# The turns of a unit's rows one step later in the scan, and the later modulation blocks on VectorE

## The chip, the cores and the metric

One core of one Trainium2 chip runs the whole program in one launch. The metric is the device time of that launch in microseconds (us). Before the change it was 1558.77 us, the median of three runs (1555.15 to 1559.71).

## The reference, cut to what matters

Two transformer blocks on 256 tokens of width 1024, in float32. The first one has a modulated norm, an RWKV mixer, neighbourhood attention and 16 experts; the second has a pooling and dilated-attention mixer, a feed-forward part and a gate, twice. The change touches two pieces of the first block.

The modulation is a product of a vector with a 1024 x 6144 matrix:

```
m_x = jnp.split(jax.nn.silu(c) @ mod_w[l] + mod_b[l], 6, axis=-1)
```

Its last four sixths are needed only behind the mixers.

The RWKV mixer runs a delta-rule scan in two directions, over 256 context tokens and then 256 latent ones, for 8 heads of 64:

```
s_kk = jnp.einsum('bhvk,bhk->bhv', s, kk_t)
s = (s * w_t[:, :, None, :]
     - s_kk[..., None] * (kk_t * a_t)[:, :, None, :]
     + v_t[..., None] * k_t[:, :, None, :])
y = jnp.einsum('bhvk,bhk->bhv', s, inp[5]) if emit else None
```

## The kernel before, in words

The scan is done in chunks of 128 tokens. A unit is one chunk `i` (0 to 3) of one direction `d` and one group `g` of four heads: 16 units. Chunks 0 and 1 are context, 2 and 3 latent; only the latter give output (`emit`). `rwkv_prep` (L642) makes a unit's rows, with the tokens on the partitions: `rr` (L688), `nb` (L699), `kh` (L703 to L705) and, with output, `pi` (L709). `turn` (L683) brings each of them into the other orientation: two 128x128 transposes on TensorE (L686) and a copy out of PSUM on ScalarE (L687). The key scaling `kk` (L664, L665) runs on GpSimd but for first chunks. `rwkv_chunk` (L714) then multiplies the turned rows (L735, with the mask on VectorE, L739), solves a triangular system by halves (`solve`, L800; its products are L835, L841 and L844, their VectorE step L837), refines it (L869 to L880) and moves the state on.

Each unit is a generator, and a `yield` ends a step. `turns` (L48) takes one step of each live generator in a round. Three slots (`SLOTS`) of units run side by side, the second 7 rounds behind the first and the third 14 (`LEAD`); slot 0 has six units, the others five. With them run `gates` (L1015), `factors` (L325) and `rwkv_out` (L892). `gates` issues one group of gate products, L119 to L121 on weights split by L127 and L128, per round, for 160 rounds; slot 0's six units have 159 steps. A unit has 25 to 29 steps, of which `rwkv_prep` has five, or six with output.

`factors` starts with `modulation_rest` (L285): eight blocks of 512 columns, 17 steps each. A block takes eight 128x512 pieces of the matrix, each loaded by SP's queue (L299) into one of three buffers. ScalarE scales the piece by its part of the vector (L300), the first into the sum, the others in place; GpSimd adds these seven to the sum (L302). Eight small products on TensorE (L307) then sum over the partitions.

What a step issues gives the order of priority; the framework puts each engine's instructions into an order of its own, by when it reckons them ready, so that the order on an engine need not be that of the text. Each engine then takes its instructions strictly in that order. The scratch tiles `kk`, `pinv`, `pe`, `pi` and `t0` have one buffer each for all slots, the rows and their turned forms one for each slot.

Of the kernel before, what the change touches and what calls it, by code (L numbers as in the profile page):

```python
# [12 lines left out]
AF = mybir.ActivationFunctionType  # L13
ALU = mybir.AluOpType
# [57 lines left out]
class Kernel:  # L72
# [212 lines left out]
    def modulation_rest(self, pool):  # L285

        nc, a = self.nc, self.a
        self.rw = self.gp.tile([P, 8, 16], F32, name="rw")
        self.rbh = self.keep.tile([P, 16], F32, name="rb")
        nc.sync.dma_start(self.rw, a["router_w"].rearrange("(k p) e -> p k e", p=P))  # L290
        rb = a["router_bias"]
        nc.sync.dma_start(self.rbh, bass.AP(tensor=rb.tensor, offset=rb.offset, ap=[[0, P], [1, 16]]))
        nc.vector.tensor_scalar(self.rbh, self.rbh, 0.5, None, op0=ALU.add)
        w = a["mod_w"][0]
        for q in range(4, 12):
            acc = pool.tile([P, 512], F32, tag="mra", name="mra", bufs=1)
            for k in range(8):
                raw = pool.tile([P, 512], F32, tag="mr", name="mr", bufs=3)
                nc.sync.dma_start(raw, w[k * P:(k + 1) * P, q * 512:(q + 1) * 512])  # L299
                nc.scalar.activation(raw if k else acc, raw, AF.Copy, scale=self.sc[:, k, 0:1])  # L300
                if k:
                    nc.gpsimd.tensor_tensor(acc, acc, raw, op=ALU.add)  # L302
                yield
                yield
            ps = self.bank()
            for j in range(4):
                nc.tensor.matmul(ps[:, j:j + 1], acc[:, j * P:(j + 1) * P], self.ones, start=True, stop=True)  # L307
            nc.vector.tensor_tensor(self.m[:, q * 4:q * 4 + 4, 0], ps[:, 0:4], self.col["mod_b"][:, q * 4:q * 4 + 4],
                                    op=ALU.add)
            yield  # L310

        self.fac = self.keep.tile([P, 32], F32, name="fac")
        nc.vector.tensor_scalar(self.fac[:, 0:8], self.m[:, 16:24, 0], 0.5, None, op0=ALU.mult)
        nc.vector.tensor_copy(self.fac[:, 24:32], self.m[:, 40:48, 0])
        nc.vector.scalar_tensor_tensor(self.fac[:, 8:16], self.m[:, 32:40, 0], 1.0, self.col["norm2_g"], op0=ALU.add,
                                       op1=ALU.mult)
        nc.vector.tensor_copy(self.fac[:, 16:24], self.m[:, 24:32, 0])
        ps = self.bank()
        nc.tensor.transpose(ps[0:32, 0:P], self.fac, self.ident)
        row = pool.tile([32, P], F32, tag="mra", name="frow", bufs=1)  # L320
        nc.vector.tensor_copy(row, ps[0:32, 0:P])
        self.facrow = self.dram.tile([32, P], F32, name="facrow")
        nc.sync.dma_start(self.facrow[:, :], row)
# [318 lines left out]
    def rwkv_prep(self, s, d, g, t, cur, first):  # L642

        nc, pool = self.nc, self.rp
        mm = nc.tensor.matmul
        tt, stt = nc.vector.tensor_tensor, nc.vector.scalar_tensor_tensor
        emit = t < 2
        c0 = t * P
        fs = slice(256 * g, 256 * g + 256)
        tmp = lambda tag: pool.tile([P, 256], F32, tag=tag, name=tag, bufs=1)  # L650
        own = lambda shape, tag, dt=F32: self.rps[s].tile(shape, dt, tag=f"{tag}{s}", name=f"{tag}{s}", bufs=1)
        flat = lambda ap: ap.rearrange("p a b -> p (a b)")
        h4 = lambda ap: ap.rearrange("p (h n) -> p h n", h=4)

        ba = self.bank()
        mm(ba[:, 0:256], self.tl[0][d][:, c0:c0 + P], self.wlb[d][:, fs], start=True, stop=True)
        mm(ba[:, 256:512], self.tl[1][d][:, c0:c0 + P], self.alb[d][:, fs], start=True, stop=True)
        th = pool.tile([P, 512], F32, tag="th", name="th", bufs=2)
        nc.scalar.activation(th, ba, AF.Tanh, scale=0.5)
        thw, tha = th[:, 0:256], th[:, 256:512]  # L660

        kk = tmp("kk")
        eng = nc.vector if first else nc.gpsimd
        eng.tensor_tensor(kk, self.zk[t][:, fs], self.kkb[:, fs], op=ALU.mult)  # L664
        eng.tensor_tensor(h4(kk), h4(kk), self.krs[:, t, 4 * g:4 * g + 4, None].to_broadcast([P, 4, 64]), op=ALU.mult)  # L665
        yield

        bi = self.bank()
        mm(bi[:, 0:256], self.cum["i", d], thw, start=True, stop=True)
        mm(bi[:, 256:512], self.cum["e", d], thw, start=True, stop=True)  # L670
        pinv, pe = tmp("pinv"), tmp("pe")
        h = -0.5 * CDEC
        nc.scalar.activation(pe, bi[:, 256:512], AF.Exp, scale=h, bias=self.off[:, 2 * d + 1:2 * d + 2])
        nc.scalar.activation(pinv, bi[:, 0:256], AF.Exp, scale=-h, bias=self.offn[:, 2 * d:2 * d + 1])
        if emit:
            pi = tmp("pi")
            nc.scalar.activation(pi, bi[:, 0:256], AF.Exp, scale=h, bias=self.off[:, 2 * d:2 * d + 1])
        yield

        rr, nb, kh = own([P, 2, 4, 64], "rr"), own([P, 256], "nb"), own([P, 256], "kh")  # L680
        krT, nkT = own([P, 2, 2, P], "krT"), own([P, 2, 2, P], "z0")

        def turn(src, dst):  # L683
            b = self.bank()
            for p in range(2):
                nc.tensor.transpose(b[:, p * P:(p + 1) * P], src[:, p * P:(p + 1) * P], self.ident)  # L686
            nc.scalar.activation(dst, b[:, 0:256].rearrange("p (a t) -> p a t", a=2), AF.Copy)  # L687
        tt(flat(rr[:, 0]), kk, pe, op=ALU.mult)  # L688
        turn(flat(rr[:, 0]), krT[:, :, 0, :])

        bt = self.bank()
        for p in range(2):
            mm(bt[:, 2 * p:2 * p + 2], thw[:, p * P:(p + 1) * P], self.half[:, d, :], start=True, stop=True)
        hv = self.sm.tile([P, 2, 2], F32, tag=f"hv{s}", name="hv", bufs=2)
        nc.scalar.activation(hv, bt[:, 0:4].rearrange("p (a b) -> p a b", b=2), AF.Exp, scale=h, bias=self.off64)
        yield
        u = tmp("t0")
        stt(u, tha, 1.0, kk, op0=ALU.add, op1=ALU.mult)
        stt(nb, u, -0.5, pinv, op0=ALU.mult, op1=ALU.mult)  # L699
        turn(nb, nkT[:, 0])  # L700
        yield
        u = tmp("t0")
        stt(u, tha, -1.0, self.kab[:, fs], op0=ALU.add, op1=ALU.mult)  # L703
        stt(u, u, 1.0, self.zk[t][:, fs], op0=ALU.add, op1=ALU.mult)
        tt(kh, u, pinv, op=ALU.mult)  # L705
        turn(kh, nkT[:, 1])
        yield
        if emit:
            tt(pi, self.zr[t][:, fs], pi, op=ALU.mult)  # L709
            turn(pi, krT[:, :, 1, :])  # L710
            yield
        cur.update(hv=hv, rr=rr, nb=nb, kh=kh, krT=krT, nkT=nkT)

    def rwkv_chunk(self, s, d, g, t, cur, state, i, y):  # L714
# [1520 lines left out]
```

## Time and profile before

| | |
|---|---|
| median of three runs | 1558.77 us |
| profiled execution: its time, its span | 1560.86 us, 1559.1 us |
| TensorE busy, share of the span | 1471.2 us, 94% |
| VectorE busy | 867.1 us, 56% |
| ScalarE busy | 673.0 us, 43% |
| GpSimd busy | 197.4 us, 13% |
| mean granted clock of TensorE | 0.964 |

The scan takes the stretch from about 220 to 600 us. PE is TensorE's matmul, PEld its weight load, DVE is VectorE, ACT ScalarE, POOL GpSimd, SP the queue that issues loads. A granted clock of 1.00 is 2.4 GHz, 0.50 is 1.2 GHz. An instruction is named by the line of the kernel that issues it; `L686` is the transpose of all turned rows, so the tile's name tells which. Idle time is what stands between two instructions of an engine, and the profile puts it down to what ended it.

### The profile page before, as it was taken

The page shows a single profiled execution, that of the slowest core. Times are in us where ns is not written, and L with a number is a line of the kernel's source. Part 1 is how long each engine was busy: PE and PEld are TensorE (multiplying, and loading weights), DVE is VectorE, ACT ScalarE, POOL GpSimd, SP SyncE. Part 2 cuts the span into 40 slices and gives each one's busy share as a digit, 9 for nine tenths or more (in the row PEclk, how much of TensorE's full clock was granted, in tenths as well). Part 3 has the DMA queues.
Part 4 walks back from the last instruction along what each step waited for, and adds up shares of the span by engine and source line. Part 5 has one row for each costly group of instructions (what it writes and reads, how often), then busy time and mean ns, then how long its engine had stood idle before and what let it go on. Part 6 is the DMA issues. An engine that isn't in the chain of part 4 may idle for free.

```text
span 1559.1 us, 26053 instructions
## 1 busy us (share of the span) xinstructions
PE 1471.2 (94%) x10562; PEld 1122.8 (72%) x10562; DVE 867.1 (56%) x1826; ACT 673.0 (43%) x1097; POOL 197.4 (13%) x253
## 2 busy tenths in 40 slices
PE   5899999989999999789999899999999999999996
PEld 3677777878777777644443358699988887998885
DVE  3678547676666776522211245564556755755555
ACT  2433556665556553210110145554444545544443
POOL 1001123332233510058000000000000000000000
PEclk9899998898899999889999999999999999999999
DMA  9412223221222234779999925355556453555542
GB/s 326 158 46 68 68 84 116 82 82 56 68 82 83 82 119 154 306 308 420 420 419 420 393 85 187 109 188 182 181 182 202 146 189 96 175 189 189 189 162 75
DMA packets 119175, 276.29 MB, mean 177 GB/s; under 512 B 8672, under 2 KB 31876, under 8 KB 107784
## 3 DMA queue, kind: packets, MB, share of 16 engines
q1 hardware_dynamic: 115608, 270.13, 49.4%
q10 hardware_dynamic: 3407, 4.42, 0.8%
q8 instruction: 85, 1.39, 0.4%
q14 instruction: 43, 0.34, 0.1%
q0 software_dynamic: 32, 0.00, 0.0%
HBM read 272.41 MB, written 2.11 MB: 176 GB/s over the span
## 4 chain that ended last, share of the span: by engine, by line
PE 54%; DVE 1%; ACT 1%; issue 0%; DVEq 0%; ACTq 0%
PE mm L119 12%; PE mm L120 12%; PE mm L121 12%; PE mm L1546 11%; PE mm L1531 1%; PE mm L1694 1%; PE mm L1610 1%; PE mm L1951 1%; PE mm L1970 1%; PE mm L1812 1%; PE mm L1924 0%; PE mm L1980 0%; PE mm L217 0%; DVE wl L184 0%; PE mm L1913 0%
## 5 line engine op out<-in xcount | busy, mean ns | idle before, releaser
L184 DVE TENSOR_TENSOR wl<-wr,wh 128x2048 fp32r<-128x2048 f32 (+2 forms) x128 | 269.1, 2103 | 206.7 <-ACT wh L183 194.2
L183 ACT ACTIVATE wh<-wr 128x2048 fp32r<-128x2048 f32 (+2 forms) x128 | 224.9, 1760 | 156.3 <-PE mm L121 105.5
L121 PE MATMUL mm<-xTh,wl 128*128 128x256 f32 x512 | 143.9, 281 | 0.0
L120 PE MATMUL mm<-xTl,wh 128*128 128x256 f32 x512 | 143.7, 281 | 0.0
L119 PE MATMUL mm<-xTh,wh 128*128 128x256 f32 x512 | 143.3, 281 | 0.0
L119 PE MATMUL mm<-wh,fh 128*128 128x512 f32 x256 | 101.4, 396 | 0.0
L121 PE MATMUL mm<-wh,fl 128*128 128x512 f32 x256 | 101.1, 395 | 0.0
L120 PE MATMUL mm<-wl,fh 128*128 128x512 f32 x256 | 101.0, 395 | 0.0
L120 PEld LDWEIGHTS mm<-xTl,wh 128*128 128x128 f32 x512 | 96.2, 188 | 0.9 <-DVE xTl L968 0.3
L119 PEld LDWEIGHTS mm<-xTh,wh 128*128 128x128 f32 x512 | 96.1, 188 | 0.7
L119 PE MATMUL mm<-wh,xTh 128*128 128x512 f32 (+1 forms) x272 | 95.8, 352 | 0.6 <-ACT big L1888 0.4
L121 PEld LDWEIGHTS mm<-xTh,wl 128*128 128x128 f32 x512 | 96.4, 188 | 0.0
L120 PE MATMUL mm<-wl,xTh 128*128 128x512 f32 (+1 forms) x272 | 92.8, 342 | 0.0
L121 PE MATMUL mm<-wh,xTl 128*128 128x512 f32 (+1 forms) x272 | 92.6, 342 | 0.0
L302 POOL TENSOR_TENSOR mra<-mra,mr 128x512 f32<-128x512 f32 x56 | 74.3, 1327 | 54.5 <-ACT mr L300 29.6
L830 ACT ACTIVATE nt<-mm 128x512 f16<-128x512 f32 x80 | 47.2, 593 | 43.9 <-PE mm L844 38.0
L119 PEld LDWEIGHTS mm<-wh,xTh 128*128 128x128 f32 x272 | 51.2, 188 | 8.4 <-issue 0.7
L967 ACT ACTIVATE yh<-hu 128x512 fp32r<-128x512 f32 x16 | 10.1, 630 | 109.0 <-DVE hu L1602 93.8
L121 PEld LDWEIGHTS mm<-wh,fl 128*128 128x128 f32 x256 | 48.1, 188 | 11.5
L119 PE MATMUL mm<-hlh,wh 128*128 128x256 f32 x152 | 56.1, 369 | 0.0
L120 PEld LDWEIGHTS mm<-wl,fh 128*128 128x128 f32 x256 | 48.1, 188 | 10.8
L119 PEld LDWEIGHTS mm<-wh,fh 128*128 128x128 f32 x256 | 48.1, 188 | 10.7
(576 smaller groups left out, 3512.1 us busy)
## 6 DMA issues: line engine op xcount, KB each, us to landing
wr<-in_w_up_dram SPq DMA_DIRECT2D x32, 1024.0 KB, 5.7
wr<-in_w_down_dram SPq DMA_DIRECT2D x32, 1024.0 KB, 5.0
wr<-in_w_in_dram SPq DMA_DIRECT2D x22, 1024.0 KB, 5.2
wr<-in_moe_w_dram SPq DMA_DIRECT2D x21, 1024.0 KB, 13.5
wh<-in_moe_w_dram SPq DMA_DIRECT2D x20, 1024.0 KB, 13.4
wl<-in_moe_w_dram SPq DMA_DIRECT2D x20, 1024.0 KB, 14.3
mr<-in_mod_w_dram SPq DMA_DIRECT2D x64, 256.0 KB, 2.9
wx<-in_moe_w_dram SPq DMA_DIRECT2D x14, 1024.0 KB, 12.8
```

The costliest lines, as they stand in the source:

```text
L119: mm(out, l.hi, r.hi, start=start, stop=False, **kw)
L120: mm(out, l.hi, r.lo, start=False, stop=False, **kw)
L121: mm(out, l.lo, r.hi, start=False, stop=stop, **kw)
L183: self.nc.scalar.activation(w.hi, raw, AF.Copy)
L184: self.nc.vector.tensor_tensor(w.lo, raw, w.hi.bitcast(F32), op=ALU.subtract)
L302: nc.gpsimd.tensor_tensor(acc, acc, raw, op=ALU.add)
L830: nc.scalar.activation(nt, v4(bz), AF.Copy)
L1531: mm(b[:, k * 256:k * 256 + 256], part[:, t, 2 * q + k, :], sel[:, t].rearrange("p j c -> p (j c)"), start=(i == 0), stop=(i == 3))
L1546: mm(b[r], lT[:, k0 + k, c0 + SLOT * j:c0 + SLOT * j + SLOT], w[:, k], start=(start and k == 0), stop=(stop and k == n - 1))
L1610: mm(acc[2 * n + k // 2][:, k % 2], part[:, k * P:(k + 1) * P], back, start=False, stop=(g == 7 and part is y.lo), skip_group_check=True)
L1694: mm(banks[t], first[:, k, t * P:(t + 1) * P], w[:, k, :], start=(k == 0), stop=False)
L1812: nc.tensor.transpose(b[:, j * P:(j + 1) * P], self.x[:, t, 512 * n + j * P:512 * n + (j + 1) * P], self.ident)
```

## The change

In `modulation_rest` the first piece of a block is scaled on ScalarE as before. Each of the other seven is taken by one VectorE operation that scales the piece and adds it to the sum; ScalarE's scaling and GpSimd's add for it are gone.

In `rwkv_prep` each `turn` is issued in the step behind the one that makes its row. The step that makes `rr` keeps the small product and `hv`; the turn of `rr` opens the next step, which makes `nb`, and so on; the turn of the last row has a step of its own. So `rwkv_prep` has six steps, or seven with output.

```
             for k in range(8):
                 ...
-                nc.scalar.activation(raw if k else acc, raw, AF.Copy, scale=self.sc[:, k, 0:1])
                 if k:
-                    nc.gpsimd.tensor_tensor(acc, acc, raw, op=ALU.add)
+                    nc.vector.scalar_tensor_tensor(acc, raw, self.sc[:, k, 0:1], acc, op0=ALU.mult, op1=ALU.add)
+                else:
+                    nc.scalar.activation(acc, raw, AF.Copy, scale=self.sc[:, k, 0:1])
                 yield
                 yield
...
         tt(flat(rr[:, 0]), kk, pe, op=ALU.mult)
-        turn(flat(rr[:, 0]), krT[:, :, 0, :])
         ...
         nc.scalar.activation(hv, ...)
         yield
+
+        turn(flat(rr[:, 0]), krT[:, :, 0, :])
         u = tmp("t0")
         stt(u, tha, 1.0, kk, op0=ALU.add, op1=ALU.mult)
         stt(nb, u, -0.5, pinv, op0=ALU.mult, op1=ALU.mult)
+        yield
         turn(nb, nkT[:, 0])
-        yield
         u = tmp("t0")
         stt(u, tha, -1.0, self.kab[:, fs], op0=ALU.add, op1=ALU.mult)
         stt(u, u, 1.0, self.zk[t][:, fs], op0=ALU.add, op1=ALU.mult)
         tt(kh, u, pinv, op=ALU.mult)
+        yield
         turn(kh, nkT[:, 1])
-        yield
         if emit:
             tt(pi, self.zr[t][:, fs], pi, op=ALU.mult)
+            yield
             turn(pi, krT[:, :, 1, :])
-            yield
+        yield
```

## Rows read from the trace of the kernel before

**Rows 1.** Windows: length; busy us (x count) PE, PEld, DVE, ACT, POOL; clock; DMA.

```profile
220.00:560.00 340.00, 317.95 (x3751) 263.70 (x3753) 231.26 (x485) 198.64 (x421) 120.64 (x129) 0.91 0.30 88
```

**Rows 2.** Timeline, GpSimd: start, length (us), what, count, idle before and what ended it.

```profile
298.94 2.94 POOL L302 TENSOR_TENSOR mra<-mra,mr 128x512 f32<-128x512 f32 x2
...
312.62 1.26 POOL L302 TENSOR_TENSOR mra<-mra,mr 128x512 f32<-128x512 f32 x1
```

**Rows 3.** Windows over the seven clumps of adds: one of them, and their sum.

```profile
468.00:483.00 15.00, 14.17 (x181) 11.76 (x179) 10.18 (x21) 10.56 (x24) 10.80 (x10) 1.00 0.47 143
...
sum 120.00, PE 106.95 PEld 89.89 DVE 86.78 ACT 71.87 POOL 78.50; mean PE 15.28 PEld 12.84 DVE 12.40 ACT 10.27 POOL 11.21
```

**Rows 4.** Windows over seven stretches between clumps: the first, and their sum.

```profile
278.00:298.00 20.00, 19.81 (x253) 16.25 (x251) 13.27 (x33) 12.31 (x30) 2.94 (x5) 1.00 0.14 41
...
sum 155.00, PE 150.58 PEld 124.58 DVE 101.03 ACT 88.04 POOL 17.54; mean PE 21.51 PEld 17.80 DVE 14.43 ACT 12.58 POOL 2.51
```

**Rows 5.** Windows over seven stretches at low clock: the longest, and their sum.

```profile
384.00:397.60 13.60, 13.60 (x101) 10.71 (x101) 8.45 (x17) 6.90 (x15) 6.41 (x5) 0.50 0.45 134
...
sum 57.90, PE 55.49 PEld 47.27 DVE 36.44 ACT 26.56 POOL 32.37; mean PE 7.93 PEld 6.75 DVE 5.21 ACT 3.79 POOL 4.62
```

**Rows 6.** TensorE's waits, 220 to 560 us: us in total, times, longest.

```profile
PE mm L686 <- DVE kh L705: 8.1, 8, 1.9
PE mm L841 <- DVE x L837: 2.8, 4, 1.6
PE mm L121 <- DVE wl L128: 2.7, 1, 2.7
PE mm L879 <- DVE rq L876: 2.5, 2, 1.9
PE mm L686 <- DVE rr L688: 2.3, 5, 0.8
```

**Rows 7.** Two lines by themselves: ns min/median/max, first and last start.

```profile
L699 DVE SCALAR_TENSOR_TENSOR nb<-t,pinv x16: 407/422/1493, 229.4 to 548.2; 128x256 f32<-128x256 f32 x16
...
L837 DVE TENSOR_TENSOR x<-mm,lv x80: 406/424/426, 245.9 to 587.2; 128x256 f16<-128x256 f32 x80
```

**Rows 8.** Timeline of VectorE and TensorE at one stall.

```profile
300.67 1.35 DVE L629 TENSOR_TENSOR sbd<-sbd,hv 64x128 f32<-64x128 f32 x1
...
302.38 0.29 DVE L629 TENSOR_TENSOR sbd<-sbd,hv 64x128 f32<-64x128 f32 x1
...
303.28 0.66 PE L686 MATMUL mm<-ident,kh 128*128 128x128 f32 x2 [1.87 <-DVE kh L705]
```

**Rows 9.** GpSimd's groups, 220 to 560 us: busy us, mean ns; idle before.

```profile
L302 POOL TENSOR_TENSOR mra<-mra,mr 128x512 f32<-128x512 f32 x56 | 74.3, 1327 | 54.5 <-ACT mr L300 29.6 <-ACT mra L300 17.4 <-PE mm L852 5.7
L664 POOL TENSOR_TENSOR kk<-zk,kkb 128x256 f32<-128x256 f32 x12 | 9.9, 823 | 63.5 <-DVE rr L688 63.5
...
L665 POOL TENSOR_TENSOR kk<-kk,krs 128x256 f32<-128x256 f32 x12 | 8.0, 667 | 0.9
```

**Rows 10.** ScalarE's scalings among its groups, 220 to 560 us.

```profile
L300 ACT ACTIVATE mr<-mr,silu_c 128x512 f32<-128x512 f32 x56 | 39.7, 718 | 20.2 <-DMA mr<-in_mod_w_dram 18.7 <-POOL mra L302 1.5
```

**Rows 11.** VectorE's groups, 220 to 560 us.

```profile
L128 DVE TENSOR_TENSOR wl<-wr,wh 128x512 fp32r<-128x512 f32 x37 | 29.7, 803 | 12.4 <-ACT wh L127 11.3 <-ACT mr L300 0.7 <-issue 0.2
...
L703 DVE SCALAR_TENSOR_TENSOR t<-th,kab 128x256 f32<-128x256 f32 x16 | 10.6, 664 | 0.1
...
L699 DVE SCALAR_TENSOR_TENSOR nb<-t,pinv 128x256 f32<-128x256 f32 x16 | 9.6, 597 | 0.0
...
L705 DVE TENSOR_TENSOR kh<-t,pinv 128x256 f32<-128x256 f32 x16 | 8.8, 552 | 0.2
```

**Rows 12.** A line of the second block by itself: ns min/median/max.

```profile
L2114 DVE SCALAR_TENSOR_TENSOR xres<-th,xres x8: 683/692/695, 1214.9 to 1548.5; 128x512 f32<-128x512 f32 x8
```

**Rows 13.** The line that takes the gate products' results: ns, first and last start.

```profile
L1051 DVE SCALAR_TENSOR_TENSOR gt<-gt,mm x4: 680/684/689, 550.1 to 579.6; 128x512 f32<-128x512 f32 x4
```

**Rows 14.** Timeline of TensorE near the end of the last chain.

```profile
595.51 0.66 PE L779 MATMUL mm<-mk,rr 128*64 128x128 f32 x8 [0.69 <-ACT rr L880]
```

More of the change, by code (lines that the diff above doesn't have):

```diff
@@ L299, in modulation_rest @@
                 nc.sync.dma_start(raw, w[k * P:(k + 1) * P, q * 512:(q + 1) * 512])
-                nc.scalar.activation(raw if k else acc, raw, AF.Copy, scale=self.sc[:, k, 0:1])
                 if k:
-                    nc.gpsimd.tensor_tensor(acc, acc, raw, op=ALU.add)
+                    nc.vector.scalar_tensor_tensor(acc, raw, self.sc[:, k, 0:1], acc, op0=ALU.mult, op1=ALU.add)
+                else:
+                    nc.scalar.activation(acc, raw, AF.Copy, scale=self.sc[:, k, 0:1])
                 yield
@@ L688, in rwkv_prep @@
         tt(flat(rr[:, 0]), kk, pe, op=ALU.mult)
-        turn(flat(rr[:, 0]), krT[:, :, 0, :])
         bt = self.bank()
@@ L696, in rwkv_prep @@
         yield
+        turn(flat(rr[:, 0]), krT[:, :, 0, :])
         u = tmp("t0")
@@ L699, in rwkv_prep @@
         stt(nb, u, -0.5, pinv, op0=ALU.mult, op1=ALU.mult)
+        yield
         turn(nb, nkT[:, 0])
-        yield
         u = tmp("t0")
@@ L705, in rwkv_prep @@
         tt(kh, u, pinv, op=ALU.mult)
+        yield
         turn(kh, nkT[:, 1])
-        yield
         if emit:
             tt(pi, self.zr[t][:, fs], pi, op=ALU.mult)
+            yield
             turn(pi, krT[:, :, 1, :])
-            yield
+        yield
         cur.update(hv=hv, rr=rr, nb=nb, kh=kh, krT=krT, nkT=nkT)
```

## The prediction

> **What bounds the kernel now.** I began with the page's slices and chain: TensorE is busy 94% of the span, and what ends last is nearly all its matmuls, so only a stage where TensorE waits or runs at its lower clock can give time back. The change touches one such stage, the scan. In the windows by stage the reader is to see that from 220 to 560 us TensorE is busy 318.0 of 340 us, so 22.0 us idle, while its granted clock averages 0.91; VectorE is busy 231.3 us, ScalarE 198.6, GpSimd 120.6 [rows 1].
>
> Next I cut the stage where the modulation adds run on GpSimd. They come in clumps: the seven of one column block lie within 15 us on GpSimd's timeline (first and last shown) [rows 2], though the text issues one every second step, that is over some 35 us. Seven clumps, 120 us in all, hold 13.0 us of TensorE's idle time (120 less 106.95), five of them at a lowered clock; the seven stretches between them, 155 us, hold 4.4 us, all at 1.00 [rows 3, 4]. Seven stretches, 57.9 us together, run at 0.50, that is 1.2 of 2.4 GHz [rows 5]. At half clock the same columns take twice as long: of the 55.5 us of matmuls there, 27.7 would vanish at full clock. Idle time and low clock are one picture: TensorE waited for VectorE's row operations, and the clock often fell around such a wait.
>
> The waits name them: TensorE stood 8.1 and 2.3 us before the transposes of L686 for kh and rr, 10.4 of its 22.0 us [rows 6]. Why VectorE is late stands in its durations. L699, with both tensors in SBUF, takes 407 ns at best and 1493 at worst; L837, the same width with one of them in PSUM, never leaves 406 to 426 [rows 7]. The timeline of one stall shows the cause: GpSimd adds from 298.94 for 2.94 us, a 64-row scaling that takes 0.29 us at 302.38 takes 1.35 at 300.67, and TensorE has stood 1.87 us for kh when it goes on at 303.28 [rows 2, 8].
>
> **The change part by part.** The sum is made against the profiled execution, 1560.86 us (span 1559.1), which lies 2.1 us above the median of 1558.77.
>
> *The modulation adds.* GpSimd loses 56 adds, 74.3 us [rows 9]. ScalarE loses 56 scalings of 718 ns, 39.7 us [rows 10]. VectorE gains 56 operations of 128x512. The gate of the second block has the same operation on the same shape, with a constant for the vector's part and GpSimd at rest: L2114, 692 ns [rows 12]. From above, L128, also with two SBUF inputs, averages 803 with collisions in it [rows 11]. That is 38.8 to 45.0 us; I take 39 us, because the adds that stretched L128 are gone.
>
> Against it stands the time that VectorE loses to GpSimd now. Against their best of about 407 ns, L703, L699 and L705 lose 16 times 257, 190 and 145 ns, 9.5 us; L128 against L2114's 692 loses 37 times 111, 4.1 us [rows 11, 12]. Of GpSimd's two-input work the adds are 74.3 of 92.2 us (with L664 and L665) [rows 9], so I put 80% of these 13.6 us down to them, 11 us; other rows of the unit lose too, so this is a floor. Net, VectorE rises by at most 28 us, to 259 of 340, 76%. It isn't the bound on average, but in the clumps it is at 86.8 of 120 now [rows 3].
>
> The Trainium skill's page "SBUF — State Buffer", section "Who interferes with whom", says that a VectorE instruction with two SBUF inputs and a GpSimd instruction that reads SBUF exclude each other, whoever starts first; the rows agree. By the same rule the new operation, also with two SBUF inputs, collides with the key scalings that stay on GpSimd, and would be the one that speaks against this edit; those are 17.9 us of work, so by it the gain shrinks and doesn't turn.
>
> *The turns.* No instruction is added or removed: 16 units move four (or three) pairs of transposes, each with its ScalarE copy, one step later, and each unit has one step more (five become six, or six become seven where output is wanted). What it gives is slack: other work is issued ahead of the transpose while VectorE finishes the row. Bounds: nothing if the engines' order doesn't follow the text, as the clumps show that it need not, and 10.4 us if every wait goes. I take 8 us, three quarters, for a wait of 1.9 us fits into a step of about 2.1 us (340 us over some 160 steps). What is late next are the waits on L837, L128 and L876, 8.0 us together [rows 6], already with a step between; they gain from the freed port and lose to 56 operations ahead of them in VectorE's queue. I set that at nothing, between -4 and +19 (half of the 39 us reaching TensorE).
>
> *The clock.* Between nothing and 27.7 us. A clump without low clock exists (468 to 483), and the longest fall, from 384 us, has TensorE busy throughout and comes ahead of its clump [rows 3, 5], so not every fall goes with the waits. I take half, 14 us.
>
> *The loads.* The 64 loads stay on SP's queue, behind the same gate loads. Now ScalarE stands 18.7 us before its scaling for them [rows 10]; that wait moves to VectorE, where the next row operation is queued behind it and then TensorE. The buffer comes free earlier, as one operation reads it in place of two. Cost 0 to 18.7 us; I take 1 us, near the low end, since VectorE's operations are spread between others and three buffers run ahead.
>
> *The end.* Slot 0 runs six units, so its last chain is issued up to six steps later, while the gate products, which fill TensorE between the chain's steps, end where they did: their last result is taken at 579.6 us [rows 13], while the last chain still runs at 595.5, where a step leaves TensorE 0.69 us idle [rows 14]. Six steps at 0.69 us cost 4 us; none if the merge products cover them, 13 us at a whole step of 2.1 us each.
>
> Sum: -8 (turns) -14 (clock) +0 (other waits) +1 (loads) +4 (end) = -17 us, so 1544 in the profiled execution and **1542 us** as the median.
>
> **The rivals.**
>
> *Clock and waits both go* (chance 0.13). The clumps come to look like the stretches between them. For: all of those have clock 1.00. Against: VectorE would then have 259 us to do in some 307 (340 less 27.7 and 10.4, plus 5). Time: 1559 - 27.7 - 10.4 + 5 = 1526 us.
>
> *The waits go, the clock stays* (0.16). For: the fall at 384 us. -8 + 5 = -3, 1556 us.
>
> *The turns stay where they were* (0.13). The order on the engines comes from a planner, as the clumps show; if the transposes are placed as before, only the freed port counts: a third of the clock's 27.7 us and none of the 8, no longer tail: 1550 us.
>
> *VectorE becomes the bound, slower* (0.16). The 56 operations stand in its queue ahead of the rows and of L837, most in the clumps, where it is busiest. If half of their 39 us reaches TensorE and the clock stays low: -8 + 4 + 19 = +15, 1574 us. It decides from 4 us on, 0.07 us for each operation. For: the new operations would bring the clumps' 86.8 us to 115 of 120 (plus 39, less 11) if all stayed in them. Against: they are the lowest in the issue order of their step, and ScalarE's queue is shorter by 40 us. The Trainium skill's "Perfetto Trace Analysis", section "Optimizing Scalar/DVE Operations", would unload a saturated VectorE, onto ScalarE or even GpSimd, but adds that the last pair shares a read port, so it may not help. By the first half of that this rival wins; the rows on L699 are its second half.
>
> **How the numbers follow.** The forecast, 1530 to 1553, has 0.42. Around 0.3%, 4.7 us, is what a measurement here can tell from no change, so "same" is 1554 to 1563. Faster: 0.42 + 0.13 + 0.13 and 0.04 of the clock-stays case, 0.72. Same: 0.12 of that case and 0.02 of the slower one, 0.14. Slower: 0.14. The range, 1522 to 1562, takes in the first three rivals; it leaves out most of the slower one and a few in a hundred below.
>
> **What would show it.** Right: no adds of L302 on GpSimd; L699 and L705 close to 410 ns at their longest, but where L664 runs; TensorE's waits at L686 under 3 us; the stretch at clock 0.50 between 220 and 560 us under 30 us; VectorE near 250 us there. Wrong: the waits at L841, L121 and L735 on VectorE grown by more than 8 us together, VectorE waiting on the loads by more than 5 us, or a scan that ends more than 5 us after its last gate product than now.

## The result, and the profile after

The changed kernel took 1533.94 us, the median of four runs (1533.32 to 1545.42), against 1559.24 us of the kernel before; the ratio is 0.9854, 95% interval 0.981 to 0.9898. The forecast was 1542 us, in a range of 1522 to 1562. The profiled execution of the changed kernel is the slowest of the five on record: 1545.42 us at a mean granted clock of 0.971, where the other four had 0.978 and took 1533.3 to 1534.8. Against the 1560.86 us of the profiled execution before it is 15.4 us shorter; between the medians lie 25.3 us.

The windows of the changed kernel, for the scan and for two pieces of its end (length; busy us of PE, PEld, DVE, ACT, POOL; clock; DMA):

```profile
220.00:560.00 340.00, 329.04 (x3967) 271.96 (x3965) 260.00 (x580) 175.10 (x386) 55.05 (x77) 0.96 0.32 97
...
554.00:572.00 18.00, 16.48 (x251) 13.75 (x249) 9.52 (x20) 8.90 (x20) 0.00 (x0) 1.00 0.86 290
572.00:583.00 11.00, 8.13 (x49) 7.02 (x49) 2.42 (x5) 1.65 (x4) 0.00 (x0) 0.53 0.01 3
```

In the same 340 us as [rows 1] TensorE is idle 11.0 us in place of 22.0, and its clock is 0.96 in place of 0.91. VectorE has 260.0 us, 29 more. The third row is worth as much attention: at the end of the scan TensorE is busy 8.1 of 11 us, at a clock of 0.53.

TensorE's waits in the changed kernel, as in [rows 6]; the turns are L687 now:

```profile
PE mm L844 <- DVE x L840: 2.1, 2, 1.3
...
PE mm L687 <- DVE kh L707: 1.2, 3, 0.8
```

The wait for kh is 1.2 us where it was 8.1. VectorE's lines in the changed kernel by themselves, as in [rows 7] (ns min/median/max; first and last start):

```profile
L701 DVE SCALAR_TENSOR_TENSOR nb<-t,pinv x16: 410/418/906, 230.0 to 528.6; 128x256 f32<-128x256 f32 x16
...
L301 DVE SCALAR_TENSOR_TENSOR mra<-mr,silu_c,mra x56: 742/746/1220, 226.9 to 493.5; 128x512 f32<-128x512 f32 x56
...
L1054 DVE SCALAR_TENSOR_TENSOR gt<-gt,mm x4: 682/686/689, 521.2 to 553.8; 128x512 f32<-128x512 f32 x4
...
L800 DVE TENSOR_TENSOR y<-y,mm x4: 404/421/422, 522.0 to 583.3; 128x256 f32<-128x256 f32 x4
```

The longest `nb` is 906 ns in place of 1493; it stands beside a key scaling, which stayed on GpSimd. The longest `kh` is 427 ns in place of 1480. The new operation has a median of 746 ns. The last two rows are the gate products' last result and the scan's last output: 553.8 and 583.3 us. Before, the first was at 579.6 [rows 13], and the second at 597.7:

```profile
L797 DVE TENSOR_TENSOR y<-y,mm x4: 414/422/422, 542.0 to 597.7; 128x256 f32<-128x256 f32 x4
```

So everything comes earlier, but the scan's end now lies 29.5 us behind the last gate product, where it lay 18.1. These two stretches as windows, before and after the change:

```profile
579.60:597.70 18.10, 17.10 (x210) 14.52 (x210) 9.39 (x18) 7.43 (x15) 0.00 (x0) 1.00 0.76 258
```

```profile
553.80:583.30 29.50, 25.11 (x302) 21.28 (x301) 12.17 (x26) 10.55 (x23) 0.00 (x0) 0.83 0.53 179
```

The longer stretch also holds more matmuls, 302 in place of 210, so the 11.4 us are not all lost. TensorE is idle 3.4 us more in it (4.4 less 1.0), and its clock is 0.83 in place of 1.00.

### The profile page after: what moved, and what is told of

It is laid out like the page before. It is cut to its first block, busy times and chain, and to the rows that moved or that the text cites. A ratio compares the mean times of both kernels' runs of the same rounds, so it can differ in the third digit from the quotient of the medians.

```text
span 1543.7 us, 25945 instructions
## 1 busy us (share of the span) xinstructions
PE 1465.2 (95%) x10562; PEld 1115.8 (72%) x10562; DVE 878.7 (57%) x1882; ACT 638.9 (41%) x1041; POOL 126.3 (8%) x197
## 4 chain that ended last, share of the span: by engine, by line
PE 54%; DVE 1%; ACT 1%; issue 0%; DVEq 0%; ACTq 0%
PE mm L119 12%; PE mm L120 12%; PE mm L121 12%; PE mm L1549 12%; PE mm L1534 1%; PE mm L1613 1%; PE mm L1697 1%; PE mm L1954 1%; PE mm L1815 1%; PE mm L1973 0%; PE mm L1927 0%; PE mm L1983 0%; PE mm L217 0%; PE mm L1916 0%; DVE wl L184 0%
## 5 line engine op out<-in xcount | busy, mean ns | idle before, releaser
L121 PEld LDWEIGHTS mm<-wh,xTl 128*128 128x128 f32 x272 | 51.2, 188 | 6.2
L120 PEld LDWEIGHTS mm<-wl,xTh 128*128 128x128 f32 x272 | 51.3, 188 | 6.0
## 6 DMA issues: line engine op xcount, KB each, us to landing
wx<-in_moe_w_dram SPq DMA_DIRECT2D x14, 1024.0 KB, 12.8
```

The source lines that it names most:

```text
L120: mm(out, l.hi, r.lo, start=False, stop=False, **kw)
L121: mm(out, l.lo, r.hi, start=False, stop=stop, **kw)
```

## The experiments

All ratios are to the kernel before, run beside each kernel on the same chip, with a 95% interval. Theory A is that the time comes from VectorE no longer being held up by GpSimd's adds ("the freed port" in the prediction and the expectations), theory B that it comes from the later turns.

**One edit at a time.** The first kernel has only the modulation edit, the second only the turns:

```
 # first: modulation_rest as changed, rwkv_prep as before
 # second: rwkv_prep as changed, modulation_rest as before
```

> The modulation edit alone, the turns as before. If the freed port is what gives the time (theory A), the longest of the unit's rows on VectorE falls from 1493 ns to under 950, TensorE's waits at the turns fall from 10.8 us to under 4, the half-clock time in the scan from 57.9 us to about 30, and the time comes out at 1535 to 1545 us. If the later turns give it (theory B), the waits at the turns stay near 10 us and the time at 1552 us or above.

> The later turns alone, the adds on GpSimd as before. Theory A: the rows on VectorE still reach 1490 ns, the half-clock time stays above 40 us, the waits at the turns shrink to about 4 us but others take their place; 1550 to 1560 us. Theory B: the waits at the turns go to about 1 us, the half-clock time to about 30; 1535 to 1545 us.

The modulation edit alone took 1530.52 us, ratio 0.9818 (0.9795 to 0.9841), below the 1535 to 1545 us of theory A. The turns alone took 1568.92, ratio 1.0068 (1.0042 to 1.0094): **slower than before**, and outside the ranges of both theories. Theory B is out, and so is my own term of 8 us for the turns, as far as the edit as it stands goes. That they cost time was not expected by theory A either, and is taken up below. The waits of the second kernel, in the scan:

```profile
PE mm L843 <- DVE x L839: 6.8, 7, 1.9
...
PE mm L686 <- DVE kh L706: 0.8, 1, 0.8
```

The turns' wait is down to 0.8 us, and the solve's wait has taken its place: 6.8 us before L843 (L841 before the change), where it was 2.8 [rows 6]. TensorE is idle 21.9 us of these 340, as before. The rows themselves are as long as ever, up to 1502 ns:

```profile
L700 DVE SCALAR_TENSOR_TENSOR nb<-t,pinv x16: 409/422/1502, 230.3 to 551.7; 128x256 f32<-128x256 f32 x16
...
L1053 DVE SCALAR_TENSOR_TENSOR gt<-gt,mm x4: 682/686/689, 544.3 to 576.9; 128x512 f32<-128x512 f32 x4
...
L799 DVE TENSOR_TENSOR y<-y,mm x4: 406/422/422, 545.1 to 606.2; 128x256 f32<-128x256 f32 x4
```

The last two rows show what else the second kernel does: the scan ends 29.3 us behind the last gate product (606.2 less 576.9). In the first kernel the same two lines start 18.2 us apart, as before, and its scan runs at full clock:

```profile
220.00:560.00 340.00, 327.74 (x4143) 271.55 (x4143) 263.26 (x594) 180.61 (x397) 53.57 (x77) 1.00 0.34 105
```

**ScalarE's part, and VectorE's price.** The third kernel scales on ScalarE as before and only adds on VectorE. The fourth leaves out the 56 operations, so seven of eight pieces are loaded and missing from the sum:

```
 # third, from the changed kernel
+nc.scalar.activation(raw if k else acc, raw, AF.Copy, scale=self.sc[:, k, 0:1])
 if k:
-    nc.vector.scalar_tensor_tensor(acc, raw, self.sc[:, k, 0:1], acc, ...)
-else:
-    nc.scalar.activation(acc, raw, ...)
+    nc.vector.tensor_tensor(acc, acc, raw, op=ALU.add)
 # fourth, from the changed kernel
-if k:
-    nc.vector.scalar_tensor_tensor(acc, raw, self.sc[:, k, 0:1], acc, ...)
-else:
+if k == 0:
     nc.scalar.activation(acc, raw, ...)
```

> As the changed kernel, but the seven pieces are scaled on ScalarE as before and only added on VectorE. VectorE's load is that of the changed kernel less 56 times some 0.06 us, ScalarE carries its 40 us again and waits for the loads again. If ScalarE's shorter queue is part of the gain, it is 3 us or more slower than the changed kernel; if the port alone counts, within 2 us of it (1532 to 1537).

> As the changed kernel, but seven of eight pieces of a block are loaded and left out of the sum. It takes 43 us off VectorE. If VectorE's new work costs TensorE nothing, as the sum had it, the time is that of the changed kernel within 3 us; if a quarter of it reaches TensorE, it is some 11 us faster, 1523 us.

The third took 1538.87 us, ratio 0.9864 (0.9837 to 0.9892); against the changed kernel's 0.9854 that is no difference that can be told. So the 40 us on ScalarE cost nothing that shows; some 4 us could hide in these intervals, and the time itself lies above the 1532 to 1537 that was expected. The fourth took 1522.92, ratio 0.9779 (0.9751 to 0.9807), 0.75% or 12 us below the changed kernel: somewhat more than a quarter of the 43 us that these operations take there. How they cost it is not shown. In the two profiled executions TensorE is idle about the same from 220 to 560 us, 10.6 us without the operations and 11.0 with them, while the clock is 0.99 and 0.96.

**Where the turns lose.** Theory C: the step that each unit has more costs, because slot 0's last chain then outlasts the gate products that fill TensorE between its steps by six steps more. Theory D: the later turns cost by themselves. One kernel takes the step out and leaves the turns behind; one adds the step alone to the modulation edit; one spreads the gate products over six more steps; and the changed kernel ran with them again.

```
 # no extra step, from the changed kernel
             turn(pi, krT[:, :, 1, :])
-        yield
         cur.update(hv=hv, ...)
 # the extra step alone, from the modulation edit
             turn(pi, krT[:, :, 1, :])
             yield
+        yield
         cur.update(hv=hv, ...)
 # gates spread, from the changed kernel: behind each block of gates, twice
+            if q % 2:
+                yield
```

> The changed kernel with the turns a step behind, but the last turn in the step of the unit's first product, so that a unit has as many steps as before. Theory C (the extra step costs, because slot 0's last chain outlives the gate products by six steps): the chain ends 18 us after the last gate product, as before the change, in place of 29; TensorE doesn't fall to half clock there; 1524 to 1532 us. Theory D (the later turns themselves cost, wherever the steps end): the time stays at 1533 us or above and the distance near 29 us.

> The modulation edit with the turns where they were, and one empty step at the end of each unit's preparation. Theory C: the chain ends 28 us or more after the last gate product in place of 18, and the time rises from 1530 to some 1536 to 1544 us. Theory D: an empty step changes nothing, 1528 to 1533 us.

> The changed kernel with six empty steps put into the gate products, so that they are issued over as many steps as slot 0's chain again. Theory C: the chain ends some 18 to 20 us after the last gate product, no half clock in that end, and 1524 to 1532 us. Theory D: 1533 us or above.

> The changed kernel as it is, on the chip of these three. 1530 to 1546 us; its profile shows whether the half-clock stretch of 13.7 us in the scan and the one of 10.2 us at its end come again. By theory C the one at the end does.

| kernel | median us | ratio, interval | last gate product to scan's end |
|---|---|---|---|
| no extra step | 1523.69 | 0.9785 (0.977 to 0.9801) | 18.1 us |
| extra step alone | 1534.28 | 0.9853 (0.9831 to 0.9875) | 29.6 us |
| gates spread | 1525.72 | 0.9827 (0.9798 to 0.9857) | 17.8 us |
| changed kernel again | 1534.98 | 0.9855 (0.9834 to 0.9876) | 29.4 us |

Theory C holds for the changed kernel. Taking the step out gives 0.7%, 10.9 us (0.9855 less 0.9785, of 1556), with intervals clear of each other, and makes the kernel with the lowest ratio of those that leave nothing out. The other two bear it out in the trace, less in the time. Adding the step alone to the modulation edit costs 0.35%, 5.4 us (0.9853 less 0.9818), but these two intervals overlap, and the 1534.28 us lie between the forecasts of the two theories. Spreading the gates brings the distance back; its median is 9 us lower, but its runs reach from 1524.73 to 1538.49, and the intervals overlap, so by the time alone this one leaves it open. All these edits also give the framework other steps to order, and no run shows what another order alone does to the time.

The clock goes with the step as well. Between the last gate product and the scan's end it is 0.83 to 0.86 in all six profiles of the kernels with the extra step and the gates as they were. It is 1.00 in the kernel before and in those without the step or with the gates spread, but for one: 0.91 in the turns without the step on the adds of before, further down.

The end of the scan in the kernel without the step, then in the one with the step alone:

```profile
547.00:565.00 18.00, 17.00 (x208) 14.63 (x209) 9.27 (x18) 7.43 (x15) 0.00 (x0) 1.00 0.71 245
```

```profile
561.00:572.00 11.00, 8.40 (x48) 7.41 (x49) 2.06 (x5) 1.57 (x3) 0.00 (x0) 0.53 0.01 1
```

Where other products (the gates' and then those of `rwkv_out`, which merges the scan's outputs) reach to the end, TensorE is busy 17.0 of 18 us at full clock. Where they don't, 11 us hold 8.4 of matmuls at a clock of 0.53. The timeline of TensorE in the changed kernel's last 11 us of the scan (start, length, what, idle before) shows the chain alone:

```profile
573.02 1.12 PE L872 MATMUL mm<-rq,tT 128*128 128x128 f32 x4 [0.47 <-ACT tT L866]
574.83 2.07 PE L878 MATMUL mm<-z,mk 128*128 128x128 f32 x8 [0.69 <-ACT z L873]
577.68 1.11 PE L882 MATMUL mm<-rq,tT 128*128 128x128 f32 x4 [0.78 <-DVE rq L879]
579.48 1.12 PE L782 MATMUL mm<-mk,rr 128*64 128x128 f32 x8 [0.69 <-ACT rr L883]
```

A wait between these products leaves TensorE 0.47 to 0.78 us idle, as the sum had it; but the product of L782, 1.12 us here at a clock of 0.53, took 0.66 in the kernel before [rows 14].

The turns without the step, on the adds of before:

> The kernel before with the turns a step behind and no extra step, the adds on GpSimd. Theory C puts the 11 us by which the turns alone were slower down to the step: the chain ends 18 us after the last gate product and the time is that of before or up to 5 us less, 1551 to 1558 us. If the later turns cost by themselves where VectorE is held up, it is slower than before, 1560 us or above.

It took 1554.69 us, ratio 0.9986 (0.9964 to 1.0007): no difference that can be told. It also lies 0.8% below the turns with the step (1.0068), so the extra step accounts for what the second kernel had lost. With the adds on GpSimd the later turns themselves neither cost nor give anything clear of the noise. The wait moves to the solve:

```profile
PE mm L842 <- DVE x L838: 8.2, 10, 1.8
```

TensorE is idle 17.5 us of the 340 here, where it was 22.0, so part of the wait did go. With the adds gone, the turns without the step (0.9785) lie below the modulation edit alone (0.9818) by 0.33%, 5 us; the two intervals overlap at their ends, so this is not settled. Where both have the extra step, the kernels with and without the later turns are the same (0.9855 and 0.9853).

**What it is on GpSimd.** Both kernels start from the one without the step and give GpSimd work that nobody needs, behind each of the 56 operations: reads in one, none in the other.

```
 # adds for nothing
+nc.gpsimd.tensor_tensor(raw, raw, raw, op=ALU.add)
 # memsets
+nc.gpsimd.memset(raw, 0.0)
+nc.gpsimd.memset(raw, 0.0)
```

> The kernel without the extra step, and behind each of the 56 VectorE operations an add of the piece to itself on GpSimd whose result nobody reads: two inputs in SBUF, as the adds of before. If GpSimd's reads are what stretched VectorE's rows (theory A), the rows reach about 1400 to 1500 ns again, half clock comes back to 20 us or more in the scan, and the time rises from 1524 to 1535 us or above. If it was the chain over ScalarE and GpSimd that cost, not the collision, the time stays within 3 us of 1524.

> The same with two memsets of the piece on GpSimd in place of the add: near the same busy time (two of some 0.53 us against 1.28) and the same hold on the buffer, but nothing read. If it is the reads that collide, the rows stay at 410 to 430 ns outside of the key scalings and the time within 3 us of 1524; if any work on GpSimd collides, or the buffer's longer hold costs, it rises as with the adds.

The adds took 1553.45 us, ratio 0.9969 (0.9946 to 0.9991): 28.6 us more than without them (0.9969 less 0.9785, of 1557), out of some 33 us that the change without the step had gained. The memsets took 1527.54, ratio 0.9814 (0.9784 to 0.9844): 4.5 us more, with overlapping intervals. From 220 to 560 us TensorE is idle 17.6 us at a clock of 0.95 with the adds, 8.6 us at 0.99 with the memsets, and 7.5 us at 0.99 with neither. GpSimd's groups and one VectorE line of the first, then of the second:

```profile
L302 POOL TENSOR_TENSOR mr<-mr 128x512 f32<-128x512 f32 x56 | 64.8, 1158 | 81.1 <-DVE mra L301 43.3 <-issue 19.3 <-PE mm L882 4.1
```

```profile
L702 DVE SCALAR_TENSOR_TENSOR nb<-t,pinv x16: 407/422/1256, 230.0 to 543.4; 128x256 f32<-128x256 f32 x16
```

```profile
L303 POOL MEMSET mr<- 128x512 f32 x56 | 29.8, 531 | 2.9
L302 POOL MEMSET mr<- 128x512 f32 x56 | 29.8, 531 | 67.4 <-DVE mra L301 60.1 <-issue 7.3
```

```profile
L703 DVE SCALAR_TENSOR_TENSOR nb<-t,pinv x16: 407/419/800, 230.0 to 517.4; 128x256 f32<-128x256 f32 x16
```

64.8 us of adds cost some 29 us; 59.6 us of memsets some 4.5 us, not clear of the noise. The rows of `nb` reach 1256 ns beside the adds, less than the 1400 that was expected; the 800 ns of the second kernel stand beside a key scaling, not a memset. This is what the Trainium skill's "SBUF — State Buffer", section "Who interferes with whom", says: a VectorE instruction with two SBUF inputs collides with what reads on GpSimd, not with what only writes.

**The rest of the collisions.** The last kernel, from the one without the step, has all key scalings on VectorE:

```
-eng = nc.vector if first else nc.gpsimd
+eng = nc.vector
```

> The kernel without the extra step, and the key scalings of the other twelve units on VectorE as well: 24 operations of some 0.42 us, 10 us more, against 17.9 us of GpSimd work that still reads. If the collisions that are left cost more than the work does, it is faster than 1524 by 1 to 4 us, and no row exceeds 430 ns but beside the bonus terms; if VectorE is the tighter engine by now, slower by 1 to 4 us.

It took 1530.02 us, ratio 0.9835 (0.9807 to 0.9863): 0.5% or 7.8 us slower than with them on GpSimd (0.9785), more than the 1 to 4 us expected of either outcome. The rows are undisturbed, and it doesn't help:

```profile
L701 DVE SCALAR_TENSOR_TENSOR nb<-t,pinv x16: 407/415/426, 231.0 to 515.8; 128x256 f32<-128x256 f32 x16
```

What costs the time is not shown. The two profiled executions lie only 1.6 us apart (1529.44 and 1527.85), with the same clock of 0.99 and nearly the same idle time of TensorE in the scan, 8.0 and 7.5 us.

## Why the prediction was right, and where it was not

The direction, its main cause and, within its range, the size were right. Two terms of the sum were wrong, and with the modulation edit set too low the errors lay on opposite sides: that the total came within 8 us of the median is in part luck. The sum was made for the profiled execution, -17 us, and there the change is -15.4; but that execution is the slowest of five, so this nearness is luck too.

- **The modulation adds and the clock**: right in mechanism, and larger than I set them. The modulation edit alone is worth 1.8%, 28 us; my sum had 14 us for the clock and 1 us against it for the loads. With it alone the scan ran at a clock of 1.00, and the turns' waits for kh and rr fell without any change to the turns, from 8.1 and 2.3 to 2.9 and 1.4 us. I had booked those to the other edit. In the changed kernel's profile about half of the low clock went, as the sum had it: 27 us at 0.50 are left in the scan of 57.9 (counted in windows of 1 us).
- **The turns, -8 us**: wrong. Alone, without the extra step, they gave nothing that can be measured (0.9986); with the adds off GpSimd, about 5 us without the extra step, not clear of the noise, and nothing with it. The reasoning failed at "what is late next": I set the change in the waits on L837 at nothing, and with the later turns the solve's wait before L841 grew from 2.8 to 8.2 us. Here most of the wait removed in front of one matmul came back in front of another, while VectorE was as late as before.
- **The end, +4 us**: the mechanism was right, the size too small. With the changed modulation the step cost 10.9 us with the later turns and 5.4 without them (intervals overlap); with the adds of before 12.8 us (1.0068 less 0.9986, of 1557). The idle time was well set: six gaps of 0.69 us, against 3.4 us more idle behind the last gate product. What I left out was the clock, 0.83 in that stretch of 29.5 us, which is at most another 5 us by an estimate (29.5 times 0.17). The rest of the 10.9 us is not located.
- **VectorE's new work**: 746 ns at the median for the operation in place of the 692 of L2114, whose factor is a constant; 43 us in all in place of 39. I set what reaches TensorE at nothing, and the rival of the slower side at half: leaving the operations out gave 12 us, more than a quarter, though TensorE's waits on VectorE are hardly longer with them (7.9 us in the scan against 6.3). The rival was wrong in the balance, since collisions stood against it, some 29 us as the idle adds measure them. That VectorE has little to spare is likely from these 12 us and from the key scalings, but the traces don't show it.
- **The loads, +1 us**: VectorE waited 2.1 us for them in the scan; small, as the sum had it, though no run shows what reached TensorE.
- **ScalarE's 40 us**: rightly counted as nothing, within the noise.

Of the signs named beforehand, the waits at the turns (1.2 us), the time at clock 0.50 (27 us) and the rows came true, and VectorE's load came near (260 against 250); the scan's end behind its last gate product, named as a sign that the prediction is wrong from 5 us on, did come, and cost what the experiments show.

What stays open is why the clock falls inside the scan. In the changed kernel's profiled execution it does so from about 286 us, for nearly 14 us. The second profile of the same kernel, at the same time (1545.45 us) and the same mean clock of 0.971, has full clock there and its longest fall from about 244 us; the scan's mean, 0.96, and the fall at the end are the same in both:

```profile
244.00:265.50 21.50, 21.50 (x197) 17.28 (x197) 9.49 (x25) 7.39 (x15) 0.44 (x1) 0.52 0.22 66
```

So the place of the long fall is not fixed by the program, and the one at the scan's end came in both. The other executions of this kernel, up to 14 us shorter at a mean clock of 0.976 to 0.980, were not profiled; what they lack is not shown.

## What to carry to other kernels

Before moving work from VectorE onto GpSimd, see whether VectorE's operations read two tensors from SBUF while GpSimd reads. In this kernel the price stood in the longest durations of such rows (1493 ns against 407), not in the busy shares. Where several generators share out the issue order, count the steps of the longest one against those of the filler: here a step more in each unit lengthened the end, where little filled it. And when a wait is to be removed by issuing the waiter later, ask what else waits for the same late engine.

## What the runs showed of the hardware that was not expected

- GpSimd work of nearly the same busy time cost some 29 us when it read SBUF (64.8 us of adds) and some 4.5 us, not clear of the noise, when it only wrote (59.6 us of memsets).
- The same fused operation on 128x512 takes 746 ns with its factor read for each partition and 692 ns with a constant [rows 12]; the plain add of the third kernel takes 684 ns on the same tiles. These are medians; that the factor makes the difference was not tested by itself.
- The granted clock falls in stretches where the profile shows TensorE busy throughout, too. In the profiled execution of the changed kernel:

```profile
285.00:300.00 15.00, 15.00 (x102) 12.17 (x103) 8.76 (x19) 6.01 (x14) 1.71 (x2) 0.54 0.29 88
```

Executions of the same program differ in their mean clock: 0.971 at 1545.42 us and 0.978 at 1533.3 to 1534.8 us.
